# A second PSUM bank for a token sum, and the first up step's weight sums on another engine, in a hybrid decoder layer

## The chip, the cores and the metric

The kernel runs on one core of one Trainium2 chip. The metric is the time of one execution on the device in microseconds (us); the median of several runs counts. The core has five engines that run side by side, each working through its own queue in order: TensorE (PE in the profile; its weight loads are PEld), VectorE (DVE), ScalarE (ACT), GpSimd (POOL) and SyncE (SP), which here issues the DMAs. All data is 32-bit. Matmuls write to PSUM, which this program divides into eight buffers of one bank (128 x 512 values) each; POOL takes its operands from SBUF only in this program.

## What is computed

One layer of a decoder, for 1024 prompt tokens and 8 sample tokens (1032 columns in all): a norm, an input projection, two recurrent mixers side by side, an output projection with a residual, and then the part that matters here, the second norm and the gated MLP:

```python
x = x + jnp.concatenate([o_a, y], axis=-1) @ w['w_out']

h = rmsnorm(x, w['norm2_w'])
gate, val = jnp.split(h @ w['w_up'], 2, axis=-1)
gate, buf_f_new = causal_dwconv(gate, buf_f, w['ffn_conv_w'], w['ffn_conv_b'])
x = x + (jax.nn.silu(gate) * val) @ w['w_down']
```

`x` has 1024 features, `w_up` is 1024 x 5632 (2816 gate and 2816 value columns). A final norm follows, and the mixers' states are outputs too.

## The kernel before, in words

Values lie with features on the 128 partitions and tokens along the free dimension, so `x` is eight tiles of 128 x 1032. Each 32-bit product is made as three matmuls: an operand is split into a rounded part ("hi", a cast by ScalarE) and the rest ("lo", a subtract by VectorE), and hi x hi, hi x lo and lo x hi are added up in PSUM.

*Output projection.* `out_job` (L1015) adds its products to `x` (L1040, VectorE, reading PSUM). For the last quarter of the input rows, in the second half of the tokens, these are 16 products of 12 matmuls; their PSUM buffers ("mm", three of them) come free when L1040 has run. `final` (L1050) then stores the finished piece to DRAM, squares it on ScalarE (L1054, L1057) and adds the squares up over the feature tiles on POOL (L1058) into `rst`. For the second half `weigh` (L1062) multiplies `x` by the norm's weight in place on ScalarE, once the store has read it.

*Second norm.* `set_norm(i, c)` (L1120) finishes the sum over features for one quarter of the tokens (258 columns): one product with a matrix of ones into a PSUM buffer `n2ms` (two matmul instructions), then `rstd_of` (L635): a reciprocal root on ScalarE (L637) and three steps on VectorE (L638, L639, L640), of which ScalarE's and the first of VectorE's read PSUM. The halves of the tokens are the two instances i = 0 and 1, and c picks the quarter within the half. The buffer comes from the tag "nx", which has one buffer (`NBANK`). The four others of that pool have the tag "mx".

*Up step.* The product with `w_up` is made with a 2 x 2 scheme of seven products per block (p1 to p7) in place of eight. `set_of(i)` (L1129) makes the seven token operands of a half: differences and sums (`comb`, L1161, on VectorE and POOL) and splits (`put`, L1153 and L1154). `up_load(j)` (L1208) loads the weights of step j (g and v, 128 columns each, of 1024 rows) and makes four weight sums of 128 x 512: v1 + v2, that + g1, g1 + v1, and the second + g2 (L1223, POOL). For j = 0 the tiles that the weights are loaded into are those of the tag "x5"; for later steps those of "ws". `up_split(j, n)` (L1233) splits the weights, two of the seven at a time (L1242 ScalarE, L1243 VectorE). There are 22 steps, j = 0 to 21; each has 14 products of 12 matmuls (`Up.mul`). p1, p7 and p3 go to "mm" buffers, p2, p4, p6 and p5 to "mx" buffers. They are read out by L1265 and L1273 (ScalarE) and L1269, L1277, L1285, L1293 and L1305 (VectorE); POOL's L1278 and L1279 stand between p7 and p3. In step 0 the order is p1, p2, p4, p6, p5, p7, p3 for the first half of the tokens and then the same for the second. There p4 is read only when p7 has been (`late`, L1293), so its buffer is held until then.

*Order.* Only TensorE's order is written out by hand: matmuls are issued in program order, and `after(n, work)` places a piece of work n matmuls later. The instructions of the other engines and the DMA queue are ordered by a scheduler when the program is built. It goes by the place in the program and by what its own estimates of durations say is ready; buffers of a tag are given out in the same way. On the chip each queue is then strictly in that order. So set_of(0) and its up_load(0) are spread over the last output products, and the two sums of the second instance are placed together:

```python
after(4, lambda: spread(set_of(1), 4))
after(93, lambda: (set_norm(1, 0), set_norm(1, 1)))
for _ in ups(0, [(name, i) for i in range(2) for name in FIRST]):
    tick()
```

93 matmuls into step 0 is behind nine of the twelve matmuls of p1 of the second half.

Of the kernel before, what the change touches and what calls it, by code (L numbers as in the profile page):

```python
# [12 lines left out]
ALU = mybir.AluOpType  # L13
# [37 lines left out]
def hybrid_layer(  # L51
# [9 lines left out]
    V, A, G, PE, SP = nc.vector, nc.scalar, nc.gpsimd, nc.tensor, nc.sync  # L61
# [9 lines left out]
    def nm(s):  # L71
        cnt[0] += 1
        return f"{s}_{cnt[0]}"
# [8 lines left out]
    def tl(tag, name, dt=F32):  # L82
        w, n = TAGS[tag]
        return (work if tag in ("hT", "big", "e", "g") else tmp).tile([P, w], dt, tag=tag, bufs=n, name=nm(name))
# [4 lines left out]
    def bank(s, tag="mx"):  # L89
        return psmx.tile([P, 512], F32, tag=tag, bufs=NBANK[tag], name=nm(s))  # L90

    def mm(out, lhsT, rhs, start=True, stop=True):
        PE.matmul(out, lhsT, rhs, start=start, stop=stop)  # L93
# [320 lines left out]
    for c, cs in enumerate(chunks):  # L414
        ps = psmm.tile([P, 512], F32, tag="mm", name=nm("dt"))
# [219 lines left out]
    def rstd_of(dst, tmp, ps, n):  # L635

        A.activation(dst, ps, AF.Abs_reciprocal_sqrt, bias=epsc, scale=1.0 / n)  # L637
        V.scalar_tensor_tensor(tmp, ps, n * EPS, dst, op0=ALU.add, op1=ALU.mult)  # L638
        V.scalar_tensor_tensor(tmp, tmp, -0.5 / n, dst, op0=ALU.mult, op1=ALU.mult)  # L639
        V.scalar_tensor_tensor(dst, tmp, 1.5, dst, op0=ALU.add, op1=ALU.mult)  # L640
# [479 lines left out]
    def set_norm(i, c):  # L1120

        cs = slice((2 * i + c) * QW, (2 * i + c + 1) * QW)
        ps = bank("n2ms", "nx")
        mm(ps[:, :QW], ones, rst[:, cs])
        rstd_of(rst[:, cs], tl("us", "nt"), ps[:, :QW], DM)

# [81 lines left out]
    def up_load(j):  # L1208
        ws = []
        for c0 in (0, DFF):  # L1210
            if j:
                t = wpool.tile([P, KT * P], F32, tag="ws", bufs=2, name=nm("ws"))
            else:
                t = tl("x5", "ws")[:, :KT * P]
            last_w[0] = SP.dma_start(t.rearrange("p (k m) -> p k m", m=P),
                                     w_up[0, :, c0 + j * P:c0 + (j + 1) * P].rearrange("(k p) m -> p k m", p=P))
            ws.append(t)
        (g1, g2), (v1, v2) = ((t[:, :512], t[:, 512:]) for t in ws)
        sums = {}

        def add(name, x_, y_):
            sums[name] = tl("t", "wt")
            G.tensor_tensor(sums[name], x_, y_, op=ALU.add)  # L1223
            return sums[name]

        p7 = add("p7", v1, v2)
        p6 = add("p6", p7, g1)
        add("p5", g1, v1)
        add("p4", p6, g2)
        sums.update(p1=g1, p2=g2, p3=v2)  # L1230
        wparts[j] = sums, {}
# [109 lines left out]
    with tc.manual_schedule(engines={mybir.EngineType.PE}):  # L1341
        finish("o4.6.0")
        after(16, lambda: set_norm(0, 0))
        after(30, lambda: set_norm(0, 1))
        after(36, lambda: spread(set_of(0), 9))
        finish("o4.6.1")
# [3 lines left out]
        up_split(0, 3)  # L1350
# [4 lines that stand above are left out]
# [30 lines left out]
        def down(w, kt, msl, acts, c):  # L1385
            q = quarters[c]
            ps = psmm.tile([P, 512], F32, tag="mm", name=nm("dn"))[:, :q.stop - q.start]
            for k in range(kt):
                hi, lo = acts[k]
                wh, wl = w(k)  # L1390
                mm(ps, wh[:, msl], hi[:, q], start=(k == 0), stop=False)
                mm(ps, wh[:, msl], lo[:, q], start=False, stop=False)
                mm(ps, wl[:, msl], hi[:, q], start=False, stop=(k == kt - 1))
                tick()
            return ps

        acts = [act_load(k) for k in range(RND)]
        for r0 in range(0, FT - RND, RND):
# [3 lines left out]
            for m in range(0, KT, 2):  # L1402
                wh, wl = wload(w_down[0, rows, m * P:(m + 2) * P], nk, 2 * P)
                for i in range(2):
# [3 lines left out]
                    for c, cs in enumerate(quarters):  # L1408
                        ps = down(lambda k: (wh[:, k, :], wl[:, k, :]), nk, slice(i * P, (i + 1) * P), acts, c)
# [14 lines left out]
    for c in (3, 0, 1, 2):  # L1424
        cs = quarters[c]
        for m in range(KT):
            ps = down(lambda k: wd[k], nk, slice(m * P, (m + 1) * P), acts, c)
# [52 lines left out]
```

## Time and profile before

| | us |
|---|---|
| median of 3 runs | 1785.31 |
| lowest and highest | 1781.18, 1785.88 |
| the profiled execution | 1784.84 |
| its span (first to last instruction) | 1782.0 |
| TensorE busy | 1723.3 |
| VectorE busy | 1132.6 |
| ScalarE busy | 823.7 |
| POOL busy | 484.4 |

The profile gives start times from the start of the span. "[3.67 <-DVE x L1040]" behind a row says that the engine was idle for 3.67 us before it, and that the end of a VectorE instruction of line 1040 that writes x ended the wait. A row with x2 merges two neighbours. L93 is the helper through which every matmul goes, so matmuls are told apart by their tiles: mm are the projections, n2ms the token sums, ua and ub the up step. In the trace of this kernel the last output products run until about 1049 us, and step 0 of the up products from there to about 1081 us.

### The profile page before, as it was taken

To read this page: it belongs to the slowest core of one execution; us is meant where nothing else is said; L and a number is where in the kernel's file an instruction comes from. 1 tells how busy PE (TensorE), PEld (TensorE's weight loads), DVE (VectorE), ACT (ScalarE), POOL (GpSimd) and SP (SyncE) were. 2 spreads that over 40 slices of the span, in tenths; PEclk is the share of its full clock that TensorE was granted. 3 is DMA by queue.
4 is the path that set the end of the run, shared out by engine and by line. 5 is a ranking of instruction groups with operands and counts; after the bars stand their busy time and mean duration, and the time that the engine had idled before them with its cause. 6 is when DMAs were issued, how large, how long until landed. Compare 5 with 4: busy or idle time off the path is not lost. (4 is left out here: it accounts for less than half of the span.)

```text
span 1782.0 us, 38562 instructions
## 1 busy us (share of the span) xinstructions
PE 1723.3 (97%) x16143; PEld 1674.7 (94%) x16143; DVE 1132.6 (64%) x2025; ACT 823.7 (46%) x1472; POOL 484.4 (27%) x481
## 2 busy tenths in 40 slices
PE   7999899999999999999999969999999999999997
PEld 6998799999999999999999969999999999999997
DVE  6667966575564565458645887766666767454545
ACT  7677688455544454445333454344333434111114
POOL 1113331220110111012000374766666664000001
PEclk9999999999999999999999999999999999999999
DMA  4144634543221222234334422222222226422212
GB/s 154 39 126 131 178 107 136 177 143 98 87 66 50 85 74 73 62 109 151 104 108 135 136 87 72 72 72 84 96 72 72 77 83 215 157 78 83 86 60 96
DMA packets 218019, 182.34 MB, mean 102 GB/s; under 512 B 13388, under 2 KB 195158, under 8 KB 217830
## 3 DMA queue, kind: packets, MB, share of 16 engines
q1 hardware_dynamic: 217558, 179.80, 32.3%
q8 instruction: 126, 2.06, 0.5%
q14 instruction: 47, 0.39, 0.1%
q0 software_dynamic: 288, 0.10, 0.0%
HBM read 141.53 MB, written 38.52 MB: 101 GB/s over the span
## 5 line engine op out<-in xcount | busy, mean ns | idle before, releaser
L93 PE MATMUL mm<-hh,wh 128*128 128x344 f32 x1248 | 405.1, 325 | 0.3 <-issue 0.2
L93 PE MATMUL mm<-hl,wh 128*128 128x344 f32 x1248 | 404.5, 324 | 0.0
L93 PE MATMUL mm<-hh,wl 128*128 128x344 f32 x1248 | 402.1, 322 | 0.0
L93 PEld LDWEIGHTS mm<-hh,wh 128*128 128x128 f32 x1248 | 235.0, 189 | 4.1 <-issue 2.6
L93 PEld LDWEIGHTS mm<-hl,wh 128*128 128x128 f32 x1248 | 235.1, 188 | 2.4 <-issue 0.9
L93 PEld LDWEIGHTS mm<-hh,wl 128*128 128x128 f32 x1248 | 235.1, 188 | 2.4 <-issue 1.7
L183 ACT CAST wh<-ws 128x1024 fp32r<-128x1024 f32 x96 | 100.5, 1047 | 245.7 <-PE dn L93 135.0
L93 PE MATMUL ub<-uh,wh 128*128 128x258 f32 x704 | 199.9, 284 | 0.0
L93 PE MATMUL ub<-ul,wh 128*128 128x258 f32 x704 | 199.9, 284 | 0.0
L93 PE MATMUL ub<-uh,wl 128*128 128x258 f32 x704 | 199.6, 283 | 0.0
L93 PE MATMUL dn<-ah,wh 128*128 128x256 f32 (+1 forms) x640 | 181.2, 283 | 1.9 <-DVE x L1410 1.9
L93 PE MATMUL dn<-al,wh 128*128 128x256 f32 (+1 forms) x640 | 180.6, 282 | 0.0
L93 PE MATMUL dn<-ah,wl 128*128 128x256 f32 (+1 forms) x640 | 180.1, 281 | 0.0
L184 DVE TENSOR_TENSOR wl<-ws,wh 128x1024 fp32r<-128x1024 f32 x96 | 126.7, 1319 | 74.8 <-ACT wh L183 74.0
L93 PE MATMUL mm<-mh,wh 128*128 128x258 f32 x512 | 147.3, 288 | 9.5 <-DVE x L1040 7.2
L93 PE MATMUL ua<-uh,wh 128*128 128x258 f32 x528 | 149.8, 284 | 0.0
L93 PE MATMUL ua<-ul,wh 128*128 128x258 f32 x528 | 149.5, 283 | 0.0
L93 PE MATMUL ua<-uh,wl 128*128 128x258 f32 x528 | 148.5, 281 | 0.0
L93 PE MATMUL mm<-ml,wh 128*128 128x258 f32 x512 | 145.7, 285 | 0.6 <-DVE ml L999 0.6
L93 PE MATMUL mm<-mh,wl 128*128 128x258 f32 x512 | 145.7, 285 | 0.0
L93 PEld LDWEIGHTS ub<-ul,wh 128*128 128x128 f32 x704 | 134.4, 191 | 0.0
L93 PEld LDWEIGHTS ub<-uh,wh 128*128 128x128 f32 x704 | 133.9, 190 | 0.0
(352 smaller groups left out, 4048.4 us busy)
## 6 DMA issues: line engine op xcount, KB each, us to landing
ws<-in_w_in_dram SPq DMA_DIRECT2D x52, 512.0 KB
ws<-in_w_up_dram SPq DMA_DIRECT2D x44, 512.0 KB
ws<-in_w_out_dram SPq DMA_DIRECT2D x24, 512.0 KB
act_d<-val SPq DMA_DIRECT2D x22, 516.0 KB
al<-act_d SPq DMA_DIRECT2D x22, 516.0 KB
ws<-in_w_down_dram SPq DMA_DIRECT2D x22, 512.0 KB
ml<-mix_d SPq DMA_DIRECT2D x48, 172.0 KB
csb<-cs_d SPq DMA_DIRECT2D x32, 256.0 KB
```

The lines of the kernel that those rows point to most:

```text
L93: PE.matmul(out, lhsT, rhs, start=start, stop=stop)
L183: A.copy(wh[:, :n], ws[:, :n])
L184: V.tensor_tensor(wl[:, :n], ws[:, :n], wh[:, :n].bitcast(F32), op=ALU.subtract)
```

## The change

The second sum of each instance (c = 1) goes to an "mx" buffer in place of the one "nx" buffer. In `up_load` the four weight sums of step 0 are made by VectorE; those of the 21 later steps stay on POOL.

```diff
     def set_norm(i, c):
 
         cs = slice((2 * i + c) * QW, (2 * i + c + 1) * QW)
-        ps = bank("n2ms", "nx")
+        ps = bank("n2ms", "mx" if c else "nx")
         mm(ps[:, :QW], ones, rst[:, cs])
         rstd_of(rst[:, cs], tl("us", "nt"), ps[:, :QW], DM)
...
         def add(name, x_, y_):
             sums[name] = tl("t", "wt")
-            G.tensor_tensor(sums[name], x_, y_, op=ALU.add)
+            (G if j else V).tensor_tensor(sums[name], x_, y_, op=ALU.add)
             return sums[name]
```

## The prediction

> **What bounds the kernel now.** I read the page first, for the engine that fills the span, then TensorE's list of waits, for where it doesn't.
>
> ```profile
> span 1782.0 us, 38562 instructions
> ...
> PE 1723.3 (97%) x16143; PEld 1674.7 (94%) x16143; DVE 1132.6 (64%) x2025; ACT 823.7 (46%) x1472; POOL 484.4 (27%) x481
> ```
>
> ```profile
> PE n2ms L93 <- DVE nt L638: 8.7, 1, 8.7
> PE mm L93 <- DVE x L1040: 7.2, 7, 3.7
> ```
>
> TensorE is busy for 97% of the span, so an edit pays only if it takes away a TensorE wait. The two longest entries of its list are the places this change touches: one wait of 8.7 us of the second token sum (n2ms), and the waits of the last output products for VectorE's sums (L1040), the longest 3.7 us. The timeline of TensorE dates them; the last bracket is the idle time and what ended it.
>
> ```profile
> 1040.16 0.39 PE L93 MATMUL mm<-mh,wh 128*128 128x258 f32 x1 [3.67 <-DVE x L1040]
> ...
> 1060.15 0.60 PE L93 MATMUL n2ms<-n2r,ones 128*128 128x258 f32 x2
> 1069.42 1.20 PE L93 MATMUL n2ms<-n2r,ones 128*128 128x258 f32 x2 [8.68 <-DVE nt L638]
> ```
>
> The table of stretches shows what TensorE's clock did around them (columns: length, busy time and count of PE, PEld, DVE, ACT, POOL, then the granted clock).
>
> ```profile
> 1034.22:1037.64 3.42, 2.27 (x19) 2.06 (x18) 0.47 (x1) 2.78 (x6) 3.42 (x4) 1.00 0.18 61
> 1037.64:1041.05 3.41, 0.89 (x7) 0.89 (x8) 3.39 (x5) 2.60 (x6) 3.41 (x3) 1.00 0.02 6
> 1041.05:1044.46 3.41, 3.41 (x19) 3.41 (x19) 2.59 (x5) 2.34 (x6) 3.41 (x5) 0.53 0.97 296
> 1061.40:1064.80 3.40, 0.00 (x0) 0.00 (x0) 3.40 (x5) 3.02 (x4) 0.00 (x0) 1.00 0.00 0
> 1069.42:1075.37 5.95, 5.95 (x26) 5.76 (x27) 3.45 (x8) 1.99 (x4) 0.00 (x0) 0.50 0.00 0
> 1111.20:1131.30 20.10, 20.10 (x170) 20.10 (x169) 13.81 (x23) 7.84 (x14) 14.48 (x15) 1.00 0.28 94
> ```
>
> The last row is a steady up step: always busy, 20.10/170 = 0.12 us a matmul. The third and fifth are the stretches after the two waits, at half clock: they lose 3.41 - 19 x 0.12 = 1.1 us and 5.95 - 26 x 0.12 = 2.8 us. So 3.7 + 1.1 + 8.7 + 2.8 = 16.3 us is the most that is to be had.
>
> What those waits hang on stands in the timelines of the other engines. VectorE:
>
> ```profile
> 1024.56 2.92 DVE L1154 TENSOR_TENSOR ul<-sm,uh 128x1032 fp32r<-128x1032 f32 x2
> 1027.40 0.41 DVE L1040 TENSOR_TENSOR x<-x,mm 128x258 f32<-128x258 f32 x1
> 1027.74 1.21 DVE L184 TENSOR_TENSOR wl<-ws,wh 128x1024 fp32r<-128x1024 f32 x1
> 1028.87 1.22 DVE L1154 TENSOR_TENSOR ul<-sm,uh 128x1032 fp32r<-128x1032 f32 x1
> 1030.02 0.74 DVE L1040 TENSOR_TENSOR x<-x,mm 128x258 f32<-128x258 f32 x2
> 1030.68 2.15 DVE L1243 TENSOR_TENSOR wl<-ws,wh 128x512 fp32r<-128x512 f32 x2
> 1032.76 0.74 DVE L1040 TENSOR_TENSOR x<-x,mm 128x258 f32<-128x258 f32 x2
> 1037.17 0.92 DVE L1243 TENSOR_TENSOR wl<-wt,wh 128x512 fp32r<-128x512 f32 x1 [3.67 <-ACT wh L1242]
> 1038.12 1.65 DVE L184 TENSOR_TENSOR wl<-ws,wh 128x1024 fp32r<-128x1024 f32 x1
> 1039.69 0.41 DVE L1040 TENSOR_TENSOR x<-x,mm 128x258 f32<-128x258 f32 x1
> ...
> 1067.13 0.41 DVE L1293 TENSOR_TENSOR fext<-us,ub 128x258 f32<-128x258 f32 x1
> 1068.52 0.42 DVE L1305 TENSOR_TENSOR val<-us,ua 128x258 f32<-128x258 f32 x1 [0.97 <-POOL us L1279]
> 1068.86 0.42 DVE L638 SCALAR_TENSOR_TENSOR nt<-n2ms,n2r 128x258 f32<-128x258 f32 x1
> ```
>
> ScalarE and POOL:
>
> ```profile
> 1034.02 0.62 ACT L1242 CAST wh<-wt 128x512 fp32r<-128x512 f32 x1 [5.10 <-POOL wt L1223]
> ...
> 1036.52 0.62 ACT L1242 CAST wh<-wt 128x512 fp32r<-128x512 f32 x1 [0.64 <-POOL wt L1223]
> ...
> 1062.74 0.37 ACT L1273 COPY us<-ub 128x258 f32<-128x258 f32 x1
> ...
> 1064.91 0.48 ACT L637 ACTIVATE n2r<-n2ms,epsc 128x258 f32<-128x258 f32 x1
> ```
>
> ```profile
> 1026.37 1.17 POOL L1314 COPY fext<-fbufT 128x16 f32<-128x16 f32 x1
> 1029.48 1.76 POOL L1223 TENSOR_TENSOR wt<-ws 128x512 f32<-128x512 f32 x1 [1.94 <-DMA x_d<-x]
> ...
> 1035.20 1.29 POOL L1223 TENSOR_TENSOR wt<-wt,ws 128x512 f32<-128x512 f32 x1
> ```
>
> The first wait, read backwards: TensorE needs the x sum at 1039.69 to free an output buffer; that stands on VectorE behind the weight subtracts at 1037.17 and 1038.12; the first of them waited 3.67 us for a cast, and the cast for POOL's last weight sum, which ended at 1036.49. VectorE is in order, so work that was ready sat behind a subtract that wasn't. The second wait: both token sums share one PSUM buffer ("nx"), which L638 frees only at 1069.28, after a long VectorE backlog.
>
> **The change, part by part.** *The bank.* With its own buffer the second sum follows the first at once; nothing else is added on TensorE. 8.68 us go. But "mx" has four buffers, and at that point the up step holds or has just returned all: p2 (free early), p6 (free early), p5 (freed by ScalarE's copy, 1062.74 + 0.37 = 1063.11) and p4 of the first half, which waits for p7 and is freed by L1293 at 1067.13 + 0.41 = 1067.54. The sum takes one, so the second half's p2, p4, p6 and p5 find three returned, and the fourth goes round. From 1060.15 + 0.6 TensorE runs the three remaining matmuls of p1, then p2 (12 x 0.12 = 1.44) until about 1062.6, waits 0.5 for p4's buffer, runs p4 until 1064.6, waits 3.0 for L1293's buffer, runs p6 until 1069.0, and then needs the sum's own buffer, freed by its L638. That can stand right behind the first one, at 1069.3 to 1069.7 (ScalarE's half is long done: the first ran at 1064.91), or behind all three of the first norm's instructions, about 0.9 later. I take the earlier, 0.7 of wait. What is late next is thus the buffer ring: 0.5 + 3.0 + 0.7 = 4.2 us of new waits against 8.68, a gain of 4.5.
>
> *The clock that follows from it.* A stretch with 0.89 of 3.41 us busy was followed by half clock, one with 2.27 was not. A wait of 3.0 us lies in one such stretch or is split over two; I count one slow stretch, 1.1 us, against 2.8 now: gain 1.7. With none it is 2.8, with the old loss 0. The Trainium skill ("TensorE: Matmul & The Clock Gate", Part 1) says that the clock falls to half after at least one idle window of some 3.4 us. The rows agree in the length, not in the word idle, since a stretch with 0.89 us of work was enough here. By the rule as written a 3.0 us wait would cost no clock, and the time would be 1.1 us lower than my sum.
>
> *The weight sums.* Four adds of 128x512 leave POOL and come to VectorE, beside the splits that it has anyway. No such add on VectorE is in the trace; the nearest row is its subtract of the same shape (min, median, max in ns):
>
> ```profile
> L1243 DVE TENSOR_TENSOR wl<-wt,wh x88: 679/1114/1792, 1037.2 to 1484.2; 128x512 fp32r<-128x512 f32 x88
> L1223 POOL TENSOR_TENSOR wt<-wt,ws x44: 1277/1735/2164, 1032.2 to 1475.9; 128x512 f32<-128x512 f32 x44
> ```
>
> I take the minimum, 0.68, because in these 7 us POOL, which ran beside the slow ones, loses just these adds: 4 x 0.68 = 2.7 us, against 3.67 us of VectorE idle time that goes. Bounds are 4 x 1.79 = 7.2 and nothing, should they fill idle time. The two subtracts at 1030.68 took 2.15 beside POOL's adds, 2 x 0.68 = 1.36 without: 0.8 back; L184 took 1.65 against 1.21: 0.4 back. That is 3.67 - 2.7 + 1.2 = 2.2 us. The catch: the first add cannot start before its weights land, 1029.48 by POOL's row, and VectorE, unlike POOL, has other work queued behind. If the adds are put in the queue behind the L1154 that ends at 1030.0, nothing is parked: 2.2. Behind the x sum that ends at 1027.81, it stands for 1.6: 0.6. Ahead of that, from 1027.4, 2.1: 0.1. POOL's own order (this add after the copy at 1026.37, although it stands ahead of that in the program) says that the schedule did not expect the weights before then, so nothing earlier. I take the mean, 1.0. Behind the adds wait the x sums, and TensorE for them: its stall comes earlier (from 1029.5 instead of 1036.5) rather than vanishing, so I leave the 1.1 of half clock where it was. VectorE is then nearly full until 1067, so this lead reaches L1293 and p6.
>
> The Trainium skill ("SBUF — State Buffer", SBUF: two separate sides) has VectorE work with two SBUF inputs and POOL work exclude each other through one shared port pair, for a whole instruction. The spread 679 to 1792 agrees. By it these adds had cost VectorE much of their time on POOL already, which favours my 0.68, but delays POOL's sums of squares by as much.
>
> The first norm's second sum moves too, but shows no wait now. **The sum:** 4.5 + 1.7 + 1.0 = 7.2 us off the profiled execution's 1784.84 (span 1782.0 and 2.84 around it): 1777.6. The median of the runs shown, 1785.31, is 0.47 above that execution, so 1778.1. My own range for this case: gain 3.9 (p5 late by 0.9 more, two slow stretches, adds at 0.1) to 11, so 1774 to 1781.4.
>
> **Rivals.** *Both waits go clean.* The schedule gives the up step buffers that are free, and VectorE gains the whole 3.67: up to 16.3 us, 1769; half way to it 1771 to 1774. For it: VectorE idles 3.67 us. Against: L1293 is behind VectorE work without a gap. Chance 0.14.
>
> *The wait only moves.* If p2 or p4, not p6, gets the buffer of the late p4, TensorE waits from about 1061 to 1067.54: 1.9 us earlier than 1069.42 and nothing saved in clock; with 1.0 from the adds 2.9: 1782.4. The code fixes four buffers, not which one. Chance 0.19.
>
> *VectorE is parked.* One mechanism: the adds sit on VectorE ahead of the x sum of 1027.40, wait 2.1 us for the weights, and run at the slow price, 7.2 us. VectorE is then 9.3 us later there, and takes back the 3.67 of idle and the 1.2: 4.4 late. L1293 follows, and eats the 4.5 of the bank edit; TensorE, stopped for about 9 us at 1027 and again later, loses the 1.1 and 2.8 of half clock once more, with 2.8 left where it was: -4.5 + 4.4 + 3.9 + 1.7 (p5 and p6 queued later still, the length of one more slow add) = 5.5 slower, 1790.8. It decides from about 5 us of VectorE lateness. Against: with POOL out of the way the slow price has no cause but the sums of squares. Chance 0.15.
>
> **How the numbers follow.** Forecast 0.52, clean 0.14, moved 0.19, parked 0.15. A difference under 0.3% (5.4 us) can't be told from none here. Faster than 1779.95: most of the forecast, 0.44, and the clean case: 0.58. Within 0.3%: the rest of the forecast and the moved wait: 0.27. Slower: 0.15. The range 1771 to 1786 holds the forecast, the moved wait and half of the clean case, with a little of a mild parked one: about 0.8.
>
> **What would show it.** In the profile after: no n2ms entry in TensorE's waits; instead ub waiting for L1293 (about 3 us) and for L638 (under 2); the weight sums as VectorE rows near 0.7 us; no 3.67 us wait before 1037, but a stall of L1040 from about 1029. If VectorE shows an idle time for a DMA near 1027, the parking is there. If the adds take over 1.2 us each, my price was wrong; if L1293 ends later than now, the second part cost what the first gained.

## The result, and the profile after

| | before | after |
|---|---|---|
| median, us | 1785.42 | 1776.53 |
| lowest and highest | 1781.18, 1787.05 | 1773.84, 1782.37 |
| runs | 10 | 10 |
| the profiled execution | 1784.84 | 1773.84 |

The ratio of after to before is 0.9961, with a 95% interval of 0.9947 to 0.9975: 7.0 us faster, between 4.5 and 9.5. The means lie 7.0 us apart, the medians 8.9. The forecast was 7.2 us. The page of the profile after, first the span and the busy times:

```profile
span 1772.1 us, 38564 instructions
...
PE 1722.1 (97%) x16143; PEld 1674.1 (94%) x16143; DVE 1131.8 (64%) x2029; ACT 824.0 (46%) x1472; POOL 477.3 (27%) x477
```

POOL has four instructions fewer, VectorE four more. TensorE's busy time fell by 1.2 us only over the whole span, so most of the gain is waiting that went away. Where it went shows in the table of stretches, cut at TensorE's own marks: the first matmul of the first n2ms, the first of step 0, of step 1, of step 2, of step 4, and the end of step 21. (The columns are the length, then the busy time and the count of PE, PEld, DVE, ACT and POOL, then the granted clock.) Before:

```profile
994.74:1049.00 54.26, 48.11 (x376) 46.80 (x374) 47.53 (x72) 27.83 (x47) 28.37 (x25) 0.97 0.40 123
1049.00:1081.62 32.62, 23.94 (x175) 23.38 (x173) 25.57 (x38) 14.18 (x25) 13.76 (x12) 0.84 0.03 9
1081.62:1101.77 20.15, 20.15 (x171) 20.15 (x170) 18.05 (x23) 8.93 (x15) 13.93 (x15) 1.00 0.25 79
1101.77:1142.35 40.58, 40.56 (x339) 40.36 (x338) 29.59 (x52) 16.64 (x29) 27.13 (x30) 1.00 0.24 79
1142.35:1504.99 362.64, 362.64 (x3027) 362.64 (x3026) 248.08 (x415) 143.34 (x252) 230.89 (x228) 1.00 0.28 92
```

The same stretches after:

```profile
993.88:1048.74 54.86, 48.43 (x376) 47.12 (x374) 49.73 (x76) 27.12 (x45) 23.64 (x23) 0.94 0.39 120
1048.74:1072.58 23.84, 21.61 (x174) 21.07 (x173) 21.97 (x35) 15.07 (x27) 10.23 (x9) 1.00 0.05 15
1072.58:1092.73 20.15, 20.15 (x170) 20.15 (x169) 18.01 (x23) 8.82 (x15) 13.43 (x14) 1.00 0.24 79
1092.73:1134.50 41.77, 40.56 (x339) 40.36 (x337) 30.82 (x55) 16.62 (x29) 28.38 (x32) 1.00 0.24 77
1134.50:1497.14 362.64, 362.64 (x3027) 362.64 (x3025) 247.78 (x415) 143.41 (x252) 229.91 (x228) 1.00 0.28 92
```

Read the first column downwards. The end of the output projection takes 0.60 us more, step 0 takes 8.78 less, and steps 2 and 3 take 1.19 more, where nothing was edited. Together 8.78 - 0.60 - 1.19 = 6.99 us less. Of the 9.97 us between the two spans the rest lies outside these stretches: 0.86 before the first n2ms, and 2.1 behind step 21. Single executions differ by that much there, so 6.99 is the figure to explain.

TensorE's timeline after has these waits (the n2ms row shows four matmuls without a gap):

```profile
1033.48 0.58 PE L93 MATMUL mm<-mh,wh 128*128 128x258 f32 x1 [4.77 <-DVE x L1040]
...
1059.89 1.04 PE L93 MATMUL n2ms<-n2r,ones 128*128 128x258 f32 x4
...
1066.06 0.39 PE L93 MATMUL ub<-uh,wh 128*128 128x258 f32 x1 [1.86 <-DVE fext L1293]
...
1068.14 0.39 PE L93 MATMUL ub<-uh,wh 128*128 128x258 f32 x1 [0.37 <-DVE nt L638]
...
1095.53 0.39 PE L93 MATMUL ua<-uh,wh 128*128 128x258 f32 x1 [1.21 <-DVE val L1305]
```

The 8.68 us are gone; p6 waits 1.86 us for L1293 and p5 0.37 for L638. The 3.67 us wait near 1036 is gone too, but a longer one of 4.77 stands at 1029 to 1033. VectorE shows why:

```profile
1028.54 0.69 DVE L1223 TENSOR_TENSOR wt<-ws 128x512 f32<-128x512 f32 x1 [0.45 <-DMA ws<-in_w_up_dram]
1029.15 1.23 DVE L1154 TENSOR_TENSOR ul<-sm,uh 128x1032 fp32r<-128x1032 f32 x1
1030.30 1.59 DVE L1223 TENSOR_TENSOR wt<-wt,ws 128x512 f32<-128x512 f32 x1
1031.81 0.68 DVE L1223 TENSOR_TENSOR wt<-ws,ws 128x512 f32<-128x512 f32 x1
1032.41 0.68 DVE L1223 TENSOR_TENSOR wt<-wt,ws 128x512 f32<-128x512 f32 x1
1033.01 0.75 DVE L1040 TENSOR_TENSOR x<-x,mm 128x258 f32<-128x258 f32 x2
...
1065.59 0.41 DVE L1293 TENSOR_TENSOR fext<-us,ub 128x258 f32<-128x258 f32 x1
1066.99 0.42 DVE L1305 TENSOR_TENSOR val<-us,ua 128x258 f32<-128x258 f32 x1 [0.99 <-POOL us L1279]
1067.33 0.75 DVE L638 SCALAR_TENSOR_TENSOR nt<-n2ms,n2r 128x258 f32<-128x258 f32 x2
```

The adds cost 0.69 + 1.59 + 0.68 + 0.68 = 3.64 us, and all four stand ahead of the two x sums for which TensorE waits. VectorE stood idle for 0.45 us until the weights landed. The one slow add ran beside a sum on POOL:

```profile
1030.19 1.14 POOL L1161 TENSOR_TENSOR sm<-x 128x516 f32<-128x516 f32 x1 [1.60 <-ACT x L1064]
```

The clock behind the two waits, after:

```profile
1033.48:1037.20 3.72, 3.72 (x17) 3.72 (x18) 3.09 (x6) 1.85 (x4) 1.79 (x2) 0.50 0.34 110
...
1066.06:1069.50 3.44, 3.07 (x23) 2.86 (x24) 2.51 (x8) 1.14 (x2) 0.90 (x2) 1.00 0.00 0
```

Half clock followed the 4.77 us, but not the 1.86.

### The profile page after: what moved, and what is told of

It reads as the page before. It is cut to its first block, busy times and chain, and to the rows that moved or that the text cites. A ratio compares the mean times of both kernels' runs of the same rounds, so it can differ in the third digit from the quotient of the medians.

```text
span 1772.1 us, 38564 instructions
## 1 busy us (share of the span) xinstructions
PE 1722.1 (97%) x16143; PEld 1674.1 (94%) x16143; DVE 1131.8 (64%) x2029; ACT 824.0 (46%) x1472; POOL 477.3 (27%) x477
## 5 line engine op out<-in xcount | busy, mean ns | idle before, releaser
L184 DVE TENSOR_TENSOR wl<-ws,wh 128x1024 fp32r<-128x1024 f32 x96 | 126.2, 1314 | 72.5 <-ACT wh L183 71.6
```

Of the source, the lines that this page charges most:

```text
L184: V.tensor_tensor(wl[:, :n], ws[:, :n], wh[:, :n].bitcast(F32), op=ALU.subtract)
```

## The experiments

**The theory.** The gain is the bank's. What is left in step 0 is the ring of four buffers, whose last member is freed by L1293, and L1293 comes when the supporting engines are through with their work, whatever TensorE does. The weight sums trade one parked queue for another. **The rivals:** the sums' lead on VectorE is what makes step 0 short; or the first wait is simply too much work for VectorE, not an order. The wait for L1305, the last reading of step 1, had to be explained besides (TensorE meets it in the second product of step 2): VectorE's own backlog, or POOL's sums of step 2.

Three measures from each timeline carry the comparison: from the start of the first n2ms to the end of the first L1293, from there to step 1, and on to step 4 (starts of the first matmuls; each ratio is against before on the same chip).

| kernel | n2ms to L1293 | L1293 to step 1 | step 1 to 4 | sum | ratio (95%) |
|---|---|---|---|---|---|
| before | 72.81 | 14.07 | 60.73 | 147.61 | 1 |
| sums only | 72.13 | 13.08 | 61.01 | 146.22 | 0.9996 (0.9987 to 1.0004) |
| bank only | 72.83 | 6.58 | 62.06 | 141.46 | 0.9962 (0.9950 to 0.9974) |
| after | 72.13 | 6.58 | 61.91 | 140.62 | 0.9961 (0.9947 to 0.9975) |
| after, run again | 72.12 | 6.57 | 62.05 | 140.74 | 0.9963 (0.9948 to 0.9977) |
| adds made twice | 74.24 | 7.43 | 61.23 | 142.91 | 0.9964 (0.9952 to 0.9975) |
| late sum | 72.13 | 4.98 | 64.70 | 141.80 | 0.9973 (0.9960 to 0.9987) |
| subtracts behind | 72.63 | 7.44 | 61.22 | 141.29 | 0.9973 (0.9958 to 0.9987) |
| L1324 on POOL | 71.87 | 6.59 | 64.83 | 143.28 | 0.9985 (0.9974 to 0.9997) |
| bank, step 2 on VectorE | 72.89 | 7.59 | 60.44 | 140.92 | 0.9964 (0.9951 to 0.9977) |
| both behind | 73.14 | 7.72 | 60.99 | 141.85 | 0.9976 (0.9966 to 0.9987) |
| all three, bank | 73.13 | 7.54 | 60.44 | 141.11 | 0.9966 (0.9951 to 0.9981) |
| all three, late sum | 73.16 | 4.99 | 61.50 | 139.65 | 0.9962 (0.9948 to 0.9976) |

### One part alone, and both

The bank alone:

```diff
-        ps = bank("n2ms", "nx")
+        ps = bank("n2ms", "mx" if c else "nx")
```

> Only the second sum of each instance goes to its own bank; the weight sums of step 0 stay on POOL. Theory A (the bank edit is nearly the whole gain): the 8.7 us wait of n2ms goes, TensorE waits about 2 to 3 us for L1293 and under 1 us for L638 instead, the half-clock stretch behind it goes if no stretch of 3.4 us is mostly idle, and the time is 6 to 9 us below the kernel before; the 3.7 us wait for L1040 near 1036 us and its half clock stay. Theory B (both edits share the gain as forecast): 5 to 6.5 us below. Theory C (the weight sums carry it): at most 3 us below.

The sums alone:

```diff
-            G.tensor_tensor(sums[name], x_, y_, op=ALU.add)
+            (G if j else V).tensor_tensor(sums[name], x_, y_, op=ALU.add)
```

> Only the four weight sums of step 0 go to VectorE; both token sums keep the one bank. Theory A: within 1.5 us of the kernel before, since the 3.7 us wait for L1040 near 1036 us is exchanged for one of 4 to 5 us near 1029 us with its own half-clock stretch, and n2ms still waits 7 to 9 us. Theory B: 1 us or more below the kernel before. Theory C: 4 us or more below. If VectorE's lateness were what decides, it would be slower by 2 us or more.

And both, the changed kernel once more:

> Both edits, the changed kernel itself, beside its two halves on one chip. Theory A: equal to the bank edit alone within 1.5 us. Theory B: 1 us or more below the bank edit alone. The sum of the two halves' differences should be its own difference within 2 us if the edits act on separate waits.

Measured: 1780.50, 1785.58 and 1780.12 us, where before took 1787.11 on that chip. The bank alone has the whole measured gain. TensorE's waits of the kernel with the sums alone:

```profile
PE n2ms L93 <- DVE nt L638: 7.8, 1, 7.8
PE mm L93 <- DVE x L1040: 7.1, 6, 5.1
```

and with the bank alone:

```profile
PE ub L93 <- DVE fext L1293: 2.2, 1, 2.2
PE ua L93 <- DVE val L1305: 1.3, 1, 1.3
```

The table's first column is the surprise: in its first five rows it is 72.8 us with the sums on POOL and 72.1 with them on VectorE. So the sums do give VectorE a lead, 0.68 us at L1293. It is too small for the timing: bank only and both differ by 0.4 us in the median, within both intervals. The second column is the bank's work: from L1293 to step 1 14.07 us become 6.58.

### The adds made twice

```diff
+            [(G if j else V).tensor_tensor(sums[name], x_, y_, op=ALU.add) for _ in range(1 if j else 2)]
```

> The changed kernel with each of the four VectorE adds of step 0 made twice (same result, 4 x 0.7 to 1.6 us more VectorE work in front of the x sums). If VectorE's place in its queue sets TensorE's stall there one for one, the stall of 4.8 us near 1029 us grows to 7.5 to 8.5 us, L1293 ends 2 to 3.5 us later, and the time is 2.5 to 5 us above the changed kernel (half clock included). If the adds only fill idle time of VectorE, it is within 1 us of the changed kernel.

On top of the change each add of step 0 is made twice. L1293 comes 2.1 us later, step 1 begins 3.0 later (81.67 against 78.70) and step 4 2.3 later; the measured ratio can't tell it from the change (1781.80 us beside 1780.12 there), so the expected 2.5 to 5 us did not show in the time. The schedule put part of the second adds behind one of the x sums, so the one wait became two:

```profile
1035.91 0.58 PE L93 MATMUL mm<-mh,wh 128*128 128x258 f32 x1 [3.80 <-DVE x L1040]
...
1039.89 0.55 PE L93 MATMUL mm<-mh,wh 128*128 128x258 f32 x1 [1.03 <-DVE x L1040]
```

VectorE's time in this stretch does reach L1293, at about half a microsecond an add, but doubling a cost does not double its wait: the queue is put in another order.

### The ring: the second sum later, and p4 later

The second sum back in "nx", placed 57 matmuls later, with the sums on VectorE:

```diff
-        after(93, lambda: (set_norm(1, 0), set_norm(1, 1)))
+        after(93, lambda: set_norm(1, 0)); after(150, lambda: set_norm(1, 1))
```

> Weight sums of step 0 on VectorE as in the changed kernel, but the second token sum takes no buffer of the up step: both sums of the second instance use the one bank again, the second one 57 matmuls later (in p7 of the second half), when the first has been read. If the ring of four buffers makes what is left of the wait in step 0, the 1.8 us wait for L1293 goes or falls under 0.7 us and step 0 lasts about 1.5 us less than the changed kernel's 23.8 us. If VectorE's lateness behind step 0 is the bound by now, the wait for L1305 one step later grows from 1.2 to between 2 and 3 us and takes that back: time within 1 us of the changed kernel. If not, 1.5 us below it.

And the change, with p4 moved behind p7, so that no buffer is held for it:

```diff
-    FIRST = ("p1", "p2", "p4", "p6", "p5", "p7", "p3")
+    FIRST = ("p1", "p2", "p6", "p5", "p7", "p4", "p3")
```

> The changed kernel with p4 behind p7 in step 0 (order p1, p2, p6, p5, p7, p4, p3), so that no buffer is held for a late p4. By the ring theory the wait for L1293 goes, as in the run with the late sum. The weight splits change their order with it (p6 and p5 second, p7 and p4 third), so the casts need the sum p6 first and the wait near 1029 us can move by about 1 us either way. Time within 2 us of the changed kernel; step 0 shorter by 1 to 2 us if the new order costs no other wait.

(The second isn't in the table, since its p4 is read elsewhere.) In both step 0 got 1.5 to 1.6 us shorter: step 1 begins 77.11 and 77.21 us behind the first n2ms, against 78.70. Without p4's hold no wait for L1293 is left; with the late sum 0.95 us of it stays, where under 0.7 was expected, since the late p4 still holds a buffer. So the ring is what remained of the wait in step 0. But TensorE then meets L1305 earlier; with the late sum

```profile
1071.03 0.36 PE L93 MATMUL ub<-uh,wh 128*128 128x258 f32 x1 [0.95 <-DVE fext L1293]
...
1100.09 0.39 PE L93 MATMUL ua<-uh,wh 128*128 128x258 f32 x1 [2.49 <-DVE val L1305]
```

and with p4 late

```profile
1100.06 0.39 PE L93 MATMUL ua<-uh,wh 128*128 128x258 f32 x1 [1.69 <-DVE val L1305]
```

The first gives all of it back (64.70 against 61.91, with half clock behind that wait), the second 1.3 of it (63.18). Measured: 1780.85 and 1780.48, with before at 1785.73; the ratio of the second is 0.9975 (0.9965 to 0.9986).

### The first wait: the subtracts behind the x sums, then the casts too

The bank alone, POOL's sums, and VectorE's subtracts of p4 and p6 (L1243) queued behind the last x sum that was issued before them:

```diff
-                            V.tensor_tensor(x_, x_, ps, op=ALU.add)
+                            last_w[1:] = [V.tensor_tensor(x_, x_, ps, op=ALU.add)]
...
-            after(76, lambda: up_split(0, 1))
+            after(76, lambda: (lambda s: (s.enter_context(tc.issue_after(last_w[1].ins)), up_split(0, 1), s.close()))(ExitStack()))
```

> The bank edit, weight sums on POOL as before, and the two VectorE subtracts of the weights p4 and p6 queued behind the x sum that was issued last when they are placed: what the weight-sum edit was to do (no x sum behind a subtract that waits for POOL), with no work moved to VectorE. If the order on VectorE and not POOL's speed makes the 3.7 us wait for L1040, that wait falls under 1 us, its half-clock stretch goes, and the output stretch lasts 3 to 5 us less than the 54 to 55 us of before. VectorE's backlog in step 0 starts earlier by 1 to 3 us, so of this 1 to 4 us stay: 8 to 11 us below the kernel before. If POOL's speed makes the wait, it moves to p4 of step 0 and the time is that of the bank edit alone.

The wait stayed, 3.26 us, where under 1 was expected. VectorE now waited at another subtract, for a cast, and that cast stood on ScalarE behind two casts that waited for POOL. VectorE and ScalarE of this kernel:

```profile
1041.19 1.23 DVE L184 TENSOR_TENSOR wl<-ws,wh 128x1024 fp32r<-128x1024 f32 x1 [4.62 <-ACT wh L183]
```

```profile
1037.09 0.62 ACT L1242 CAST wh<-wt 128x512 fp32r<-128x512 f32 x1 [5.32 <-POOL wt L1223]
```

So the same block stands in two queues. With both put right, by the same means for the casts and the last square (L1057):

```diff
+            last_w[2:] = [A.activation(sq, x_, AF.Square)]
...
+            after(76, lambda: (lambda s: (s.enter_context(tc.issue_after(last_w[1].ins)), s.enter_context(tc.issue_after(last_w[2].ins)), up_split(0, 1), s.close()))(ExitStack()))
```

> The bank edit alone, with the splits of p4 and p6 of step 0 (VectorE's subtracts and ScalarE's casts) queued behind the last x sum and the last square of the output projection. Theory (the 3.7 us wait for L1040 near 1036 us is nothing but ready work queued behind casts and subtracts that wait for POOL's weight sums, and whoever leaves one of these two queues as it is only moves it): the L1040 wait and its half clock stretch go, the stretch from the first n2ms to the first ua gets 3 to 5 us shorter than the 55.2 of the bank edit alone, and part of it, up to 3 us, comes back as a longer wait for L1293 in step 0, because the splits now run later on VectorE; 1 to 4 us less in the span. Rival (the wait is for VectorE's or ScalarE's plain amount of work there): the wait stays within 1 us of 3.7, somewhere between 1025 and 1040 us.

No wait for L1040 above 0.90 us is left, and no half clock in the output projection, and step 0 begins 48.75 us behind the first n2ms, 6.5 less than with the bank alone (55.22). The theory of the blocked order holds against "too much work". And yet nothing is won: TensorE arrives early, and waits 3.3 us for POOL's sums of squares, which the first n2ms of the second instance needs:

```profile
PE n2ms L93 <- POOL n2r L1058: 3.6, 2, 3.3
```

```profile
1059.24 1.71 POOL L1223 TENSOR_TENSOR wt<-wt,ws 128x512 f32<-128x512 f32 x1
1060.92 3.28 POOL L1058 TENSOR_TENSOR n2r<-n2r,n2sq 128x258 f32<-128x258 f32 x3
```

The last of them stand on POOL behind the weight sums of step 1. L1293 ends 73.14 us behind the first n2ms, 0.3 later than with a TensorE that had lost 6.5 us on the way. Measured: 1779.33 (before there 1785.73) and 1781.88 (before there 1786.85).

### The wait for L1305

The change, with the product L1324 of step 0 moved from VectorE to POOL:

```diff
-        V.tensor_tensor(val[:, :NT], val[:, :NT], ext[:, :NT], op=ALU.mult)
+        (V if j else G).tensor_tensor(val[:, :NT], val[:, :NT], ext[:, :NT], op=ALU.mult)
```

> The changed kernel with the last product of step 0 (L1324, 2.3 us on VectorE, which idles 2.0 us ahead of it) made by POOL. If the wait of 1.2 us for L1305 that the bank edit brings in step 1 is VectorE's backlog, it goes, steps 2 and 3 last 40.6 us again instead of 41.8 us, and the time is about 1 us below the changed kernel. If it comes from POOL (L1279 ahead of L1305), it stays or grows, since POOL gets about 3 us more.

VectorE had less to do and the wait grew, from 1.2 to 2.62 us; POOL and TensorE:

```profile
1090.11 2.87 POOL L1324 TENSOR_TENSOR val<-val,fext 128x1032 f32<-128x1032 f32 x1
```

```profile
1102.48 0.39 PE L93 MATMUL ua<-uh,wh 128*128 128x258 f32 x1 [2.62 <-DVE val L1305]
```

The amount of work on VectorE is thus not what makes the wait. ScalarE's cast of the second sum waits for POOL in this kernel:

```profile
1094.26 0.62 ACT L1242 CAST wh<-wt 128x512 fp32r<-128x512 f32 x1 [4.44 <-POOL wt L1223]
```

POOL's sums of step 2 start when their weights have landed, before and after:

```profile
1091.11 1.30 POOL L1223 TENSOR_TENSOR wt<-ws 128x512 f32<-128x512 f32 x1 [6.06 <-DMA ws<-in_w_up_dram]
```

```profile
1083.25 1.29 POOL L1223 TENSOR_TENSOR wt<-ws 128x512 f32<-128x512 f32 x1 [6.15 <-DMA ws<-in_w_up_dram]
```

That is 9.49 us behind the start of step 1 before (1081.62), and 10.67 after (1072.58): TensorE got ahead of them by 1.2 us. The counter-test makes the sums of step 2 on VectorE, with the bank edit:

```diff
-            G.tensor_tensor(sums[name], x_, y_, op=ALU.add)
+            (V if j == 2 else G).tensor_tensor(sums[name], x_, y_, op=ALU.add)
```

> The bank edit alone, and in addition the weight sums of step 2 (not of step 0) are made by VectorE instead of POOL. Theory (the 1.2 to 1.3 us that TensorE waits for L1305 at the end of step 1 come through POOL, whose sums of step 2 start about 1.2 us later behind step 1's start than in the kernel before, and delay the casts and subtracts that VectorE does in order ahead of L1305): that wait falls below 0.5 us, and steps 2 and 3 of the up product take about 40.6 to 40.9 us instead of the 41.8 of the bank edit alone; 0.7 to 1.2 us less than that kernel in the span, 1779.3 us where that one has 1780.5. Rival (VectorE itself is late there, and four adds more make it later): the wait grows to 3 us or more, and steps 2 and 3 take 43 us or more, with half clock.

The wait is gone, and steps 2 and 3 run without a pause (last row; step 0 above it):

```profile
1053.16:1079.42 26.26, 23.23 (x174) 22.46 (x173) 24.53 (x38) 14.01 (x25) 13.83 (x12) 0.94 0.04 12
...
1099.57:1139.86 40.29, 40.29 (x338) 40.29 (x337) 28.44 (x50) 16.63 (x29) 26.74 (x30) 1.00 0.25 80
```

Both tests agree that L1305 is late through POOL's adds. The first L1305 of step 1 starts 21.29 us behind the start of step 1 before, 22.49 after, 23.91 with L1324 on POOL and 20.29 with the sums of step 2 on VectorE. How the adds delay it is not one thing. With L1324 on POOL, a cast and then a subtract wait for them. In the profile after, VectorE pauses for no more than 0.14 us between L1324 at 1083.33 and L1305 at 1095.07; there its instructions run slower beside the adds (last section), and this piece of its queue, too, starts 1.1 us later against TensorE than before (10.75 us behind step 1 instead of 9.66). What each of these is worth the tests don't part. In the time the gain doesn't show (1780.50, before 1786.85); in the profile step 0 lost 1.0 us to half clock that the run with the bank alone did not lose.

### Three in one

```diff
+            last_w[2:] = [A.activation(sq, x_, AF.Square)]
...
+            (V if j == 2 else G).tensor_tensor(sums[name], x_, y_, op=ALU.add)
...
+        after(93, lambda: set_norm(1, 0)); after(150, lambda: set_norm(1, 1))
```

> One buffer for all token sums again, with the second sum of the second instance placed 150 matmuls into step 0 instead of 93; POOL makes the sums of step 0 and VectorE those of step 2; the splits of p4 and p6 are queued behind the last x sum and square. Theory (the three costs are independent: the ring of buffers in step 0, the parked queues near 1036 us, POOL's sums of step 2): no L1040 wait above 1 us, step 0 near 22 to 24 us, steps 2 and 3 near 40.6 to 41, the span 2 to 6 us below that of the kernel with both edits of the change. Rival (what is taken from one wait returns at the next, since VectorE is full from 1020 to 1070 us): the span within 1 us of the kernel with both edits.

> As the run with the late second sum in one buffer, but with the bank edit in its place: second sum in a buffer of the up step, VectorE's sums in step 2 only, the splits of p4 and p6 of step 0 queued behind the last x sum and square. Theory (independent costs): as that run, but with the wait for L1293 in step 0 of 2 to 3 us, so step 0 near 24 to 26 us; the span 1 to 4 us below the kernel with both edits. Rival (full VectorE): within 1 us of it.

These combine the edits shown above: the queueing of the casts and subtracts, step 2's sums on VectorE, and the late sum (first) or the bank (second); step 0's sums stay on POOL. Measured: 1778.50 and 1779.89, before 1786.85; ratios of 0.9962 and 0.9966 beside the change's 0.9961 and 0.9963. The theory of three independent costs falls: L1293 ends where it did (73.1 us), and what the first wait gave is waited for at n2ms. In its profile the version with the late sum is 1.0 us ahead of the change at step 4 (139.65 against 140.62); the timing can't tell them apart. No version beat the change measurably.

## Why the prediction was right, and where its terms were off

**What bounds the kernel.** Right: no steady stretch changed (362.64 us for steps 4 to 21 in both), only the waits did.

**The bank: 4.5 us forecast, 6.45 measured.** The mechanism came as forecast: no n2ms entry, p6 waiting for L1293 and p5 for L638, with the two L638 side by side. The new waits were 1.86 + 0.37 = 2.23 us instead of 4.2. The step that was mis-sized is when TensorE and the returning buffers meet. The forecast took L1293 and ScalarE's copy of p5 at the times of before; in the profile after both come 1.5 us earlier, L1293 at 1065.59 and the copy at 1061.21:

```profile
1061.21 0.37 ACT L1273 COPY us<-ub 128x258 f32<-128x258 f32 x1
```

The early start of this execution (0.86 us) moves TensorE as well, so the times from the first n2ms are what counts. By these L1293 ends 0.68 us earlier than before, the sums' lead, and TensorE is ready for p6 0.46 later than forecast (70.32 us instead of 69.86). That is 0.60 from the longer end of the output projection and about 0.4 for the second sum's own matmuls, which the forecast left out, less the 0.5 for which p4 was to wait and didn't. Together they are the 1.14 by which p6 waited less: 1.86, where 3.0 was forecast. With the bank alone it waits 2.2.

**The clock: 1.7 forecast, 2.3 measured.** One slow stretch was counted in step 0, and none came. TensorE's busy time in step 0 fell from 23.94 to 21.61. It was close: the bank alone waited 2.2 us there and kept its clock, but the kernel with step 2's sums on VectorE, the same program up to there, waited 2.72 us with half clock behind it, and needed 7.59 us from L1293 to step 1 instead of 6.58. By the Trainium skill's rule ("TensorE: Matmul & The Clock Gate", Part 1), which asks for a whole idle window of some 3.4 us, neither the change nor that run would have lost its clock; the profile after agrees and that run does not.

**The weight sums: 1.0 forecast, 0.68 of lead.** Price and place were wrong, the sum was near. The adds took 3.64 us, not 2.7, as one of them ran beside POOL; the Trainium skill's rule on the shared port ("SBUF — State Buffer", SBUF: two separate sides) agrees with that 1.59 us beside 0.68. Nor was the place one of the three that were weighed: the first add stands behind the L184 of 1026.88, with 0.45 us parked, and the other three behind the L1154 that follows it. As forecast, the stall moved ahead to 1029 and half clock stayed; its size is 4.77 instead of 3.67. The end of the output projection got 0.60 us longer, 0.28 of it idle time and 0.32 busy time at the lower granted clock (0.94 instead of 0.97 in the tables above), while VectorE got 0.68 ahead. On TensorE the term is thus -0.60 where it stands, and the lead is in the shorter wait for L1293, already counted above.

**Not foreseen: 1.19 us given back at L1305.** "What is late next" was followed as far as the end of step 0 and no further. TensorE arrives earlier, POOL's sums of step 2 and VectorE's work beside them come 1.1 to 1.2 us later relative to it, and the two tests with L1324 and with step 2's sums show that POOL's adds are on the path. So 6.45 + 2.33 - 0.60 - 1.19 = 6.99. The total of the forecast was right partly by luck: a gain that was forecast too low met losses that weren't forecast. The low end of its range is mis-added: its terms give 4.5 - 0.9 + 0.6 + 0.1 = 4.3, not 3.9; the measured time lies inside either way.

**The rivals.** *Clean* fell: 1.86 us of ring wait remained and the first wait grew. *The wait only moves* fell: TensorE ran p2 and p4 without a pause. *Parked* fell, although VectorE was parked: 0.45 us and one slow add, against the 9.3 us that it needed; even with the adds made twice L1293 came only 2.1 us later.

## What to carry to other kernels

When a wait goes, follow TensorE to the next thing it needs from every other engine, past the end of the stage: here removed waits came back in part at L1293, at L1305 and at n2ms, because the supporting engines keep their own time. Look for a mark that doesn't move when TensorE's waits do (here the end of L1293, 71.9 to 73.2 us behind the first n2ms in all kernels of the table but that with the adds doubled, whether TensorE got to step 0 6.5 us earlier or not); an edit could pay here only if it moved that mark, or shortened what TensorE still had to do behind it, and even that came back where the next need was late (the late sum, at L1305). The bank edit paid because it moved the second token sum and 27 matmuls from behind the mark to ahead of it.

## What the runs showed of the hardware

- Waits of much the same length were followed by half clock or not: in step 0, 1.86 us (after), 2.2 (bank alone), 2.45 (L1324 on POOL) and 2.40 (all three, late sum) were not, 2.32 (all three, bank), 2.33 (both behind), 2.54 (adds twice) and 2.72 (subtracts behind, and step 2 on VectorE) were. It cost about 1.0 us each time (7.4 to 7.7 against 6.58 from L1293 to step 1). The traces show what decides: in each of them the granted clock changes only at the marks of a grid of 3.41 us, and TensorE's busy time in one such window sets the clock of the next. The 2.72 us of the run with step 2 on VectorE lie almost wholly in one window (first row; the next window is the second):

```profile
1069.49:1072.90 3.41, 1.00 (x8) 1.01 (x9) 2.42 (x5) 1.87 (x5) 2.26 (x2) 1.00 0.00 0
1072.90:1076.31 3.41, 3.41 (x17) 3.18 (x17) 3.41 (x10) 1.14 (x2) 0.00 (x0) 0.50 0.02 5
```

The 2.45 us with L1324 on POOL are split over two, and the second of these has 1.60 us of work:

```profile
1069.77:1073.19 3.42, 1.60 (x12) 1.49 (x12) 2.43 (x5) 1.28 (x3) 1.91 (x2) 1.00 0.01 2
1073.19:1076.60 3.41, 3.01 (x25) 2.93 (x25) 3.41 (x10) 1.52 (x3) 0.00 (x0) 1.00 0.02 5
```

Between 990 and 1140 us of the 14 traces, the 23 windows at full clock with at most 1.48 us of work (after, from 1027.24) were all followed by half clock, and none of the 558 with at least 1.54 (sums only, from 1029.50) was. So the 1.86 us of the change kept the clock wherever the grid lay (at least 1.55 us of any window stay busy), while for 2.2 us it was a matter of where the grid fell.
- In the pairs looked at here, a two-input instruction of VectorE and one of POOL that start within 0.2 us of each other do not run at full speed side by side: the one that starts first keeps its time. The product L1324 (128 x 1032) takes VectorE 1.23 us with POOL idle, in the run with step 2's sums on VectorE. In the profile after it started 0.08 us behind POOL's add of 1083.25 (1.29 us, shown above) and took 2.30:

```profile
1083.33 2.30 DVE L1324 TENSOR_TENSOR val<-val,fext 128x1032 f32<-128x1032 f32 x1 [1.97 <-ACT fext L1323]
```

With the bank alone it started 0.13 us ahead of the same add; it took 1.23, and the add 2.25:

```profile
1086.88 1.23 DVE L1324 TENSOR_TENSOR val<-val,fext 128x1032 f32<-128x1032 f32 x1 [1.96 <-ACT fext L1323]
```

```profile
1087.01 2.25 POOL L1223 TENSOR_TENSOR wt<-ws 128x512 f32<-128x512 f32 x1 [6.35 <-DMA ws<-in_w_up_dram]
```

- What lies behind step 21 took 274.8 to 277.5 us in the single profiles, among them the two of the same kernel at 274.9 and 275.1. It doesn't follow the edits; its cause stays open.
